# Weight group 3 rounded one step earlier, and last outputs stored as whole rows, in a two-layer decoder step

## The chip, the cores and the metric

The kernel runs on one core of a Trainium2 chip. The metric is device time of one execution in microseconds (us), the median over runs; lower is better. The engines are TensorE (PE in the profile; its weight loads are PEld), VectorE (DVE), ScalarE (ACT), GpSimd (POOL) and SyncE (SP), each with its own instruction queue in order. DMAs are issued from the queues of SP, ACT and POOL and run on 16 DMA engines.

## The reference

One inference step of a two-layer decoder, for two groups of requests that use the same weights: a prompt of 1024 tokens with 16 meta tokens ahead of it, and 8 samples of 8 tokens with state and cache. Layer one is an mLSTM, layer two an attention with forget gates; each is followed by a SwiGLU FFN, and a root-mean-square norm ends it. Everything is in f32. Cut to what matters here, the mixer's projection and the end:

```python
def rmsnorm(x, g):
    r = lax.rsqrt(jnp.mean(x * x, axis=-1, keepdims=True) + EPS)
    return x * r * g

def mlstm_mixer(xn, ..., w_in, b_ig, b_fg, mh_g, w_out):     # xn = rmsnorm(h, norm_a)
    p = xn @ w_in              # (T, 1024) @ (1024, 3088)
    q = heads(p[..., :HK]) * DK_A ** -0.5                    # HK = 512
    k = heads(p[..., HK:2 * HK])
    v = heads(p[..., 2 * HK:2 * HK + HV])                    # HV = 1024
    og = p[..., 2 * HK + HV:2 * HK + 2 * HV]
    gi = p[..., 2 * HK + 2 * HV:2 * HK + 2 * HV + H_A]       # gate columns, H_A = 8
    gf = p[..., 2 * HK + 2 * HV + H_A:]
    ...

def run_trunk(h, ...):
    for l in range(DEPTH):
        h = h + mixer_l(rmsnorm(h, ...))
        h = h + swiglu(rmsnorm(h, norm_ffn[l]), w_gate_up[l], w_down[l])
        ...
    y = rmsnorm(h, norm_final)
    return y, ...              # y_prompt is (1, 1024, 1024)
```

## The kernel before

All 1104 tokens (64 of the samples, 16 meta tokens, 1024 of the prompt) are held with features on the partitions, in nine tiles: tile 0 has the 80 first tokens, tiles 1 to 8 have 128 tokens of the prompt each (`TT`). Every product is made of three matmuls: each f32 operand is split into a high part, rounded to the f32r format by a cast on ACT, and a low part, the remainder, subtracted on DVE (`split`, lines 270 to 272; `mm3`, lines 191 to 195). So a weight has to be loaded, cast on ACT and subtracted on DVE before TensorE can use it.

**The start** is `values_a` (line 632): the value columns of `w_in`, in four groups `c` of 256 columns. The order of PE, SP, DVE and ACT is written out by hand there. A group is loaded in two halves `z` of 512 rows each (`fetch`, two raw buffers, tag `wraw`), and each half is split by `halve(c, z, ks)`, whose `ks` are those of its four blocks of 128 rows that are to be done: for each block one cast on ACT that also multiplies by the norm's gain (line 665) and one multiply-subtract on DVE (line 666). Group 3 also carries the 16 gate columns, so it is 272 columns wide; the gate columns of a half are split behind its last block (line 669, by the helper in lines 271 and 272). A product `values(c, i)` of group `c` and tile `i` has eight k-steps of three matmuls; the first four read half 0, the last four half 1, with the gate columns.

The first loop runs over steps `i` from 0 to 13 (`LAG` is 5). In a step, as far as tiles are left, TensorE makes group 0's product of tile `i`, then the eight transposes of tile `i + 2` (line 733); from step 5 on it then makes group 3's product of tile `i - 5`. ACT casts tile `i + 2`, writes out the product of group 0 with the factor `rr` (line 683), squares tile `i + 2` and takes its root (lines 751 and 752). DVE makes the low parts of tile `i + 2` (line 272) and copies its transposes (`keep`, line 745, four buffers `hs`, stored by POOL's queue), then a reciprocal for the next step (line 773). Loads of `x` tiles run ahead on SP's queue. Group 3's halves are loaded ahead of the loop and in step 0; `halve(3, ...)` stands behind the squares in steps 2 to 5, two blocks each. Group 1's loads, in step 5, take over group 3's raw buffers.

**The end** is `Tail` (line 2005): the last three tiles, 6 to 8, of the prompt. `finish` makes the last products of the second FFN, sums squares, transposes the three tiles back (feature blocks 0 to 3 into the PSUM tile `lo[x]`, blocks 4 to 7 into `hi[x]`), takes root and reciprocal for all three, and calls `out` for x = 0, 1, 2. `out` scales `lo` on DVE, with the final gain, and `hi` on ACT, and stores each of them. As place for the scaled outputs it uses the tile's own columns of `H`, where 512 features of a token lie as four pieces of 128, `T` = 1104 columns apart. All stores are issued on SP's queue.

Of the kernel before, what the change touches and what calls it, by code (L numbers as in the profile page):

```python
# [11 lines left out]
AF = mybir.ActivationFunctionType  # L12
ALU = mybir.AluOpType
# [4 lines left out]
P = 128  # L18
D = 1024
# [8 lines left out]
TT = [(0, T0)] + [(T0 + P * i, T0 + P * (i + 1)) for i in range(SEQ // P)]  # L28
# [603 lines left out]
def values_a(self, v, kp, gates, w_in, c3):  # L632

    nc, I = self.nc, self.I
    E = mybir.EngineType
# [6 lines left out]
    with ExitStack() as cw, self.pool("ppA0", bufs=4, space=PSUM) as pp:  # L642
# [3 lines left out]
        rr, ss = (xr.tile([P, NT], F32, name=nm, bufs=1) for nm in ("rr", "ss"))  # L646
# [3 lines left out]
        def fetch(c, z, queue=nc.sync):  # L650
            c0 = 2 * HA * DK + 256 * c
            raw = raws[c, z] = wr.tile([P, 4, 256], F32, name=self.uid("wraw"), tag="wraw", bufs=2)
            queue.dma_start(raw, w_in[4 * z * P : 4 * z * P + 4 * P, c0 : c0 + 256].rearrange("(k p) n -> p k n", p=P))

        def halve(c, z, ks=range(4)):
            raw = raws[c, z]
            n = 272 if c == 3 else 256
            hi, lo = W[c, z] = W.get((c, z)) or [wr.tile([P, 4 * n], F32R, name=self.uid(nm), tag=nm, bufs=4).rearrange(
                "p (k n) -> p k n", k=4) for nm in ("whi", "wlo")]
            if c == 2:  # L660
                self.split(raw, hi, lo)
                return
            for k in ks:
                y = hi[:, k, :256]
                nc.scalar.activation(y, raw[:, k], AF.Copy, scale=G(4 * z + k))
                nc.vector.scalar_tensor_tensor(out=lo[:, k, :256], in0=raw[:, k], scalar=G(4 * z + k),
                                               in1=y.bitcast(F32), op0=ALU.mult, op1=ALU.subtract)
            if c == 3 and ks[-1] == 3:
                self.split(gw[:, 4 * z : 4 * z + 4], hi[:, :, 256:], lo[:, :, 256:])

        def values(c, i, half=None):
            n, m = 272 if c == 3 else 256, size(i)
            ps = pp.tile([P, 512], F32, name=self.uid("tmps"), tag="mm0")
            for k in range(KT):
                if half and k == 4:
                    half()
                h, l = self.x_tile(i, k)
                wh, wl = W[c, k // 4]
                self.mm3(ps[:m, :n], h, l, wh[:, k % 4], wl[:, k % 4], k == 0, k == KT - 1)

            def out():
                r = 1.0 if c == 2 else rr[:m, i : i + 1]
                nc.scalar.activation(v(i)[:m, 2 * c : 2 * c + 2, :DV],
                                     ps[:m, :256].rearrange("p (h d) -> p h d", h=2), AF.Copy, scale=r)
                if c == 3:
                    nc.scalar.activation(gates[:m, i, :], ps[:m, 256:272], AF.Copy, scale=r)
            return out

        def reload(i):
            n, (t0, t1) = size(i), TT[i]  # L690
            y = hr[i] = xr.tile([P, KT, P], F32, name=f"hr{i}", tag="hr")
            nc.sync.dma_start(y[:, :, :n], self.hD[:, :, t0:t1])

        def spread(i):
            rb = xr.tile([P, P], F32, name=f"rb{i}", tag="rb")
            hr[i] = hr[i], rb
            nc.sync.dma_start(rb, rD[i].partition_broadcast(P))
# [21 lines left out]
        def load(i):  # L719
            x = xin[i] = cell(f"xin{i}")  # L720
            if i == 0:
                nc.sync.dma_start(x[:NS], I["x_sample"].rearrange("b t d -> (b t) d"))
                nc.sync.dma_start(x[NS:T0], I["meta_tokens"])
            else:
                nc.sync.dma_start(x, I["x_prompt"][0, (i - 1) * P : i * P, :])

        def turn(i):
            n = size(i)
            for g in range(2):
                ps = xps[i, g] = tp.tile([P, 4, P], F32, name=self.uid("xps"), tag="xps")  # L730
                for k in range(4):
                    f = 4 * g + k
                    nc.tensor.transpose(ps[:, k, :n], xin[i][:n, f * P : (f + 1) * P], self.ident[:n, :n])

        def halves(i):
            n, (t0, t1) = size(i), TT[i]
            for g in range(2):
                ks = slice(4 * g, 4 * g + 4)
                self.split(xps[i, g][:, :, :n], xh[:, ks, t0:t1], xl[:, ks, t0:t1])

        def keep(i):
            n, (t0, t1) = size(i), TT[i]
            hs = lp.tile([P, KT, P], F32, name="hs", bufs=4)
            for g in range(2):
                nc.vector.tensor_copy(hs[:, 4 * g : 4 * g + 4, :n], xps.pop((i, g))[:, :, :n])
            nc.gpsimd.dma_start(self.hD[:, :, t0:t1], hs[:, :, :n])

        def squares(i):
            n = size(i)
            x = xin.pop(i)[:n]  # L750
            nc.scalar.activation(x, x, AF.Square, accum_out=ss[:n, i : i + 1])
            nc.scalar.activation(rr[:n, i : i + 1], ss[:n, i : i + 1], AF.Sqrt, scale=1.0 / D, bias=self.eps[:n])
# [17 lines left out]
        for i in range(NT + LAG):  # L770
            if i < NT:
                out = values(0, i, None if i else lambda: turn(1))
                nc.vector.reciprocal(rr[: size(i), i : i + 1], rr[: size(i), i : i + 1])
            if i == 0:
                halves(1)
                nc.vector.tensor_tensor(out=gw, in0=gw, in1=self.gain[:, G_A : G_A + KT].unsqueeze(2).broadcast_to([P, KT, 16]),
                                        op=ALU.mult)
                rows = xr.tile([P, P], F32, name="growsF", tag="rb")[: NG - G_F]
                self.gains(rows)
                squares(1)  # L780
                keep(1)
                load(5)
                fetch(3, 1)
            if i + 2 < NT:
                turn(i + 2)
                halves(i + 2)
            if i < NT:
                out()
            if i + 2 < NT:
                squares(i + 2)  # L790
                keep(i + 2)
            if i + 6 < NT:
                load(i + 6)
            if 2 <= i < 6:
                halve(3, i // 2 - 1, range(2 * (i % 2), 2 * (i % 2) + 2))
            if i == 5:
                fetch(1, 0)
                fetch(1, 1)
                for x in range(3):
                    reload(x)  # L800
            if i == 7:
                ps = tp.tile([P, 4, P], F32, name="gpsF", tag="xps").rearrange("p a b -> p (a b)")
                nc.tensor.transpose(ps[:, : NG - G_F], rows, self.ident[: NG - G_F, : NG - G_F])
                nc.vector.tensor_copy(self.gain[:, G_F:], ps[:, : NG - G_F])
            if i == NT - 1:
                nc.gpsimd.dma_start(rD.rearrange("i p -> p i"), rr)
                for x in range(3):
                    spread(x)
            if 0 <= i - (NT + LAG - 3) < 2:
                halve(1, i - (NT + LAG - 3))  # L810
            if i >= LAG:
                values(3, i - LAG)()
# [69 lines left out]
@_add(Net)  # L882
def phase_a(self, vt):
    nc, I, O = self.nc, self.I, self.O
    w_in = I["w_in_a"][0]
    qkD = self.dram.tile([8, P, T], F32, name="qkD")
    ogD = self.dram.tile([8, P, T], F32, name="ogD")
# [1117 lines left out]
class Tail:  # L2005
# [57 lines left out]

    def out(self, x, lo, hi):
        net, i = self.net, DONE[3][x]
        nc, t0, t1 = net.nc, *TT[i]
        for g, ps in enumerate((lo, hi)):
            o = net.H[:, 4 * g : 4 * g + 4, t0:t1]
            y, rr = ps.rearrange("p (k n) -> p k n", k=4), self.r[:, 1, x : x + 1]
            if g:  # L2070
                nc.scalar.activation(o, y, AF.Copy, scale=rr)
            else:
                nc.vector.scalar_tensor_tensor(out=o, in0=y, scalar=rr, in1=net.sq[:, :512].rearrange(
                    "p (k n) -> p k n", k=4), op0=ALU.mult, op1=ALU.mult)
            nc.sync.dma_start(net.O["y_prompt"][0, (i - 1) * P : i * P, g * 512 : g * 512 + 512].rearrange(
                "p (k n) -> p k n", k=4), o)

    def finish(self, acc, groups):
        net = self.net
# [963 lines left out]
```

## Time and profile before

| | |
|---|---|
| median of 3 runs | 2831.09 us (2831.01 to 2832.83) |
| the profiled execution's own time | 2833.03 us |
| its span, first to last instruction | 2831.2 us |
| mean granted TensorE clock | 0.994 |
| busy: PE, DVE, ACT, POOL | 2760.9, 1797.8, 1177.0, 837.0 us |
| moved by DMA | 474.03 MB, mean 167 GB/s |

The profile has a page with sums, and views of the trace behind it: groups of instructions by line, waits (who waited for whom), a timeline in order of time (start in us from the span's start, length, engine, line, operation, output and inputs, count, and in brackets the idle time before it and what ended that), busy time in chosen stretches, and the DMAs. The end of a matmul is modelled, and neighbours overlap; the pace is read from starts. A "q" behind an engine's name marks its instruction queue.

### The profile page before, as it was taken

The numbers are of one execution on the slowest core, as the hardware profiler recorded it, in microseconds if no ns is written. First come the engines' busy times: TensorE is split into PE (matmuls) and PEld (weight loads), VectorE is DVE, ScalarE is ACT, GpSimd is POOL, SyncE is SP. The second block draws the span as 40 slices with busy tenths as digits, with TensorE's granted clock in tenths as the row PEclk, the third lists the DMA queues.
The fourth block names the chain that finished last, engine by engine and source line by source line (L and its number), as shares of the span: only waits on it lengthen the run. The fifth ranks groups of instructions, "written<-read, shape, count | busy, mean of one in ns | idle before, by whom it ended". The sixth has DMA issues, their size and how long they took to land. (4 is left out here: it accounts for less than half of the span.)

```text
span 2831.2 us, 60542 instructions
## 1 busy us (share of the span) xinstructions
PE 2760.9 (98%) x23543; PEld 2649.8 (94%) x23543; DVE 1797.8 (63%) x4025; ACT 1177.0 (42%) x2299; POOL 837.0 (30%) x1316
## 2 busy tenths in 40 slices
PE   8989999999999999999999999999999999999998
PEld 8989889999999999999999888777899999999998
DVE  4632565888887665563455444777388888765656
ACT  5422453432322333443444445777343323323345
POOL 3122233132332332124352202554313223323111
PEclk9989999999999999999999999999999999999999
DMA  6666547245554375545443676442524555527556
GB/s 197 170 186 172 144 125 254 91 145 164 174 172 144 115 247 171 194 143 174 139 170 131 234 277 227 153 143 86 157 80 131 175 174 165 161 90 233 182 194 214
DMA packets 438737, 474.03 MB, mean 167 GB/s; under 512 B 41158, under 2 KB 364994, under 8 KB 437426
## 3 DMA queue, kind: packets, MB, share of 16 engines
q1 hardware_dynamic: 388050, 321.30, 36.9%
q0 software_dynamic: 43904, 143.18, 15.3%
q10 hardware_dynamic: 6496, 5.68, 0.6%
q8 instruction: 185, 3.03, 0.5%
q14 instruction: 102, 0.84, 0.1%
HBM read 322.84 MB, written 147.21 MB: 166 GB/s over the span
## 5 line engine op out<-in xcount | busy, mean ns | idle before, releaser
L1614 PE MATMUL m<-xh,slot 128*128 128x276 f32 x2752 | 540.5, 290 | 1.8 <-ACT fs L1643 1.8
L1614 PEld LDWEIGHTS m<-xh,slot 128*128 128x128 f32 x2752 | 439.6, 188 | 3.6 <-ACT fs L1643 2.2
L1614 PE MATMUL m<-xl,slot 128*128 128x276 f32 x1376 | 397.1, 289 | 0.0
L1614 PEld LDWEIGHTS m<-xl,slot 128*128 128x128 f32 x1376 | 258.7, 188 | 0.0
L193 PE MATMUL tmps<-slot,xh 128*128 128x256 f32 (+2 forms) x864 | 243.1, 281 | 0.0
L195 PE MATMUL tmps<-slot,xl 128*128 128x256 f32 (+2 forms) x864 | 240.6, 278 | 0.0
L194 PE MATMUL tmps<-slot,xh 128*128 128x256 f32 (+2 forms) x864 | 240.5, 278 | 0.0
L272 DVE TENSOR_TENSOR slot<-slot,slot 128x1024 fp32r<-128x1024 f32 x124 | 162.7, 1313 | 61.3 <-ACT slot L271 59.6
L271 ACT CAST slot<-slot 128x1024 fp32r<-128x1024 f32 x124 | 129.5, 1045 | 140.9 <-PE m L1614 111.7
L194 PEld LDWEIGHTS tmps<-slot,xh 128*128 128x128 f32 (+1 forms) x864 | 159.2, 184 | 0.1
L195 PEld LDWEIGHTS tmps<-slot,xl 128*128 128x128 f32 (+1 forms) x864 | 158.6, 184 | 0.0
L193 PEld LDWEIGHTS tmps<-slot,xh 128*128 128x128 f32 (+1 forms) x864 | 158.4, 183 | 0.2
L193 PE MATMUL mmA<-xh,whi 128*128 128x384 f32 (+1 forms) x384 | 135.7, 353 | 0.0
L194 PE MATMUL mmA<-xl,whi 128*128 128x384 f32 (+1 forms) x384 | 128.6, 335 | 0.0
L195 PE MATMUL mmA<-xh,wlo 128*128 128x384 f32 (+1 forms) x384 | 128.2, 334 | 0.0
L272 DVE TENSOR_TENSOR slot<-vA,slot 128x1024 fp32r<-128x1024 f32 (+1 forms) x59 | 82.2, 1396 | 32.6 <-ACT slot L271 31.5
L272 DVE TENSOR_TENSOR slot<-Ht,slot 128x1024 fp32r<-128x1024 f32 (+1 forms) x59 | 82.0, 1393 | 32.7 <-ACT slot L271 31.6
L271 ACT CAST slot<-Ht 128x1024 fp32r<-128x1024 f32 (+1 forms) x59 | 60.9, 1036 | 95.5 <-PE m L1614 86.5
L271 ACT CAST slot<-vA 128x1024 fp32r<-128x1024 f32 (+1 forms) x59 | 60.8, 1035 | 95.5 <-PE m L1614 86.5
L1718 DVE TENSOR_TENSOR ws<-ws 128x128 f32<-128x128 f32 x264 | 93.7, 355 | 8.9
L2865 ACT ACTIVATE s<-s,nb 128x272 f32<-128x272 f32 (+7 forms) x126 | 98.9, 786 | 0.0
L2900 ACT COPY th<-tp 128x768 f32<-128x768 f32 (+1 forms) x80 | 73.6, 920 | 53.6 <-PE tp L2892 30.5
(808 smaller groups left out, 8665.9 us busy)
## 6 DMA issues: line engine op xcount, KB each, us to landing
ws<-in_w_down SPq DMA_DIRECT2D x176, 128.0 KB, 2.7
sD<-ws SPq DMA_DIRECT2D x176, 128.0 KB, 2.2
slot<-sD SPq DMA_DIRECT2D x40, 512.0 KB, 4.4
slot<-in_w_gate_up SPq DMA_DIRECT2D x36, 512.0 KB, 3.9
kp<-in_cache_k SPq DMA_DIRECT2D x32, 512.0 KB, 6.2
vp<-in_cache_v SPq DMA_DIRECT2D x32, 512.0 KB, 5.1
vA<-in_w_gate_up SPq DMA_DIRECT2D x26, 512.0 KB, 4.5
Ht<-in_w_gate_up SPq DMA_DIRECT2D x26, 512.0 KB, 3.9
```

What stands on the lines that cost most here:

```text
L193: mm(ps, sh, mh, start=first, stop=False)
L194: mm(ps, sh, ml, start=False, stop=False)
L195: mm(ps, sl, mh, start=False, stop=last)
L271: self.nc.scalar.copy(hi, src)
L272: self.nc.vector.tensor_tensor(out=lo, in0=src, in1=hi.bitcast(F32), op=ALU.subtract)
L1614: nc.tensor.matmul(u.ps[h, b], w[p][:, k], x[q][:, k], start=first and k == i == 0, stop=k == 3 and i == 2, skip_group_check=True)
L1718: tt(out=o, in0=a, in1=b, op=ALU.subtract)
L2865: nc.scalar.activation(ss[z, u], ss[z, u], AF.Exp, bias=nb[:, z : z + 1], accum_out=sm[:, u, z : z + 1])
L2900: nc.scalar.copy(th.rearrange("p x z (u h q) -> p h (x z u) q", h=2, q=64)[:, :, :n], pt[:, :, :n])
```

## The change

Two edits. In `values_a`, `halve(3, ...)` runs in steps 1 to 4 instead of 2 to 5, with the same blocks in the same order. In `Tail.out`, both halves of a tile's output are written side by side into row `x` of `H` (1024 neighbouring elements on each partition), and one DMA stores the whole rows of 4 KB; for x = 2 it is issued on ACT's queue. ACT's half is now issued ahead of DVE's. A line in `phase_a` only gives a name that nothing uses.

```diff
-            if 2 <= i < 6:
-                halve(3, i // 2 - 1, range(2 * (i % 2), 2 * (i % 2) + 2))
+            if 1 <= i < 5:
+                halve(3, (i - 1) // 2, range(2 * (1 - i % 2), 4 - 2 * (i % 2)))
...
 def phase_a(self, vt):
     nc, I, O = self.nc, self.I, self.O
+    E = mybir.EngineType
...
     def out(self, x, lo, hi):
         net, i = self.net, DONE[3][x]
-        nc, t0, t1 = net.nc, *TT[i]
-        for g, ps in enumerate((lo, hi)):
-            o = net.H[:, 4 * g : 4 * g + 4, t0:t1]
-            y, rr = ps.rearrange("p (k n) -> p k n", k=4), self.r[:, 1, x : x + 1]
-            if g:
-                nc.scalar.activation(o, y, AF.Copy, scale=rr)
-            else:
-                nc.vector.scalar_tensor_tensor(out=o, in0=y, scalar=rr, in1=net.sq[:, :512].rearrange(
-                    "p (k n) -> p k n", k=4), op0=ALU.mult, op1=ALU.mult)
-            nc.sync.dma_start(net.O["y_prompt"][0, (i - 1) * P : i * P, g * 512 : g * 512 + 512].rearrange(
-                "p (k n) -> p k n", k=4), o)
+        nc, rr = net.nc, self.r[:, 1, x : x + 1]
+        y = net.H[:, x, :D]
+        nc.scalar.activation(y[:, 512:], hi, AF.Copy, scale=rr)
+        nc.vector.scalar_tensor_tensor(out=y[:, :512], in0=lo, scalar=rr, in1=net.sq[:, :512], op0=ALU.mult, op1=ALU.mult)
+        (nc.scalar if x == 2 else nc.sync).dma_start(net.O["y_prompt"][0, (i - 1) * P : i * P], y)
```

## The prediction

> **What bounds the kernel now.** I read the page first, then TensorE's waits, then the timeline around the longest wait that the change can touch, then the clock in windows, and last the end of the trace.
>
> ```profile
> PE 2760.9 (98%) x23543; PEld 2649.8 (94%) x23543; DVE 1797.8 (63%) x4025; ACT 1177.0 (42%) x2299; POOL 837.0 (30%) x1316
> ```
>
> TensorE (PE) is busy for 98% of the span. Time can only come from its waits, from a lower granted clock, or from the two ends. Among its six longest waits of the whole run is this one (us in total, times, longest):
>
> ```profile
> PE tmps L193 <- ACT whi L271: 2.7, 1, 2.7
> ```
>
> ```profile
> 35.07 0.29 PE L195 MATMUL tmps<-whi,xl 128*80 128x272 f32 x1
> 38.11 0.51 PE L193 MATMUL tmps<-whi,xh 128*80 128x272 f32 x1 [2.75 <-ACT whi L271]
> ```
>
> The second row (start, length, instruction, idle before it) is the fifth k-step of the first product of weight group 3. It reads the second half of that group's weights, and the last write into that half is a narrow cast of the gate columns. ScalarE (ACT) makes it here, the third and, after the dots, the end of the fourth part of the group (columns: start, length):
>
> ```profile
> 33.54 0.90 ACT L665 ACTIVATE whi<-wraw,gain 128x256 fp32r<-128x256 f32 x2
> ...
> 37.83 0.23 ACT L271 CAST whi<-gw 128x64 fp32r<-128x64 f32 x1
> ```
>
> So TensorE arrives at 35.20 (one pace of 0.13 after 35.07) and finds the cast ending at 38.06. The wait also costs clock. In this table the columns are stretch, length, busy us (instructions) of PE, PEld, DVE, ACT, POOL, granted clock, DMA share, GB/s:
>
> ```profile
> 33.98:37.39 3.41, 1.38 (x11) 1.11 (x9) 3.32 (x7) 3.38 (x9) 0.84 (x1) 1.00 1.01 317
> 37.39:40.81 3.42, 2.69 (x11) 2.39 (x12) 1.12 (x5) 0.66 (x3) 0.85 (x1) 0.50 0.86 264
> 40.81:44.22 3.41, 3.41 (x18) 3.41 (x17) 0.00 (x0) 0.63 (x2) 0.00 (x0) 0.50 0.08 24
> 44.22:47.63 3.41, 3.41 (x30) 3.41 (x30) 0.98 (x2) 1.60 (x4) 0.00 (x0) 1.00 0.65 182
> 255.84:259.26 3.42, 1.93 (x13) 1.64 (x11) 0.71 (x2) 0.49 (x1) 3.42 (x7) 1.00 0.29 77
> 259.26:262.67 3.41, 2.78 (x23) 2.81 (x24) 1.39 (x4) 0.00 (x0) 3.41 (x5) 1.00 0.37 90
> ```
>
> After a window in which TensorE was busy 1.38 of 3.41 us (40%) the clock fell to 0.50 for two windows; after one with 1.93 of 3.42 (56%) it did not fall.
>
> **Part 1: the weights one step earlier.** The four calls of `halve(3, ...)` go from steps 2 to 5 to steps 1 to 4. Each issues two casts on ACT and two multiply-subtracts on DVE; the second and the fourth also split the gate columns. None issues a DMA. Nothing is added or removed.
>
> What the wait costs in this execution comes from the transposes, which start each step's second part:
>
> ```profile
> 25.59 1.04 PE L733 MATMUL xps<-ident,xin 128*128 128x128 f32 x8
> 29.20 1.04 PE L733 MATMUL xps<-ident,xin 128*128 128x128 f32 x8
> 32.82 1.04 PE L733 MATMUL xps<-ident,xin 128*128 128x128 f32 x8
> 45.39 1.04 PE L733 MATMUL xps<-ident,xin 128*128 128x128 f32 x8
> ```
>
> ```profile
> 64.41 0.48 ACT L683 ACTIVATE vA<-tmps,rr 128x256 f32<-128x256 f32 x1 [2.39 <-PE tmps L195]
> ...
> 67.44 0.48 ACT L683 ACTIVATE vA<-tmps,rr 128x256 f32<-128x256 f32 x1 [2.39 <-PE tmps L195]
> ```
>
> A step of transposes and one plain product is 32.82 - 29.20 = 3.62; a product of group 3 is 67.44 - 64.41 = 3.03. At full clock the last transposes would start at 32.82 + 3.62 + 3.03 = 39.47; they start at 45.39. The stall costs 5.92: 2.75 of wait, about 3.2 of half clock.
>
> Will the weights be there at 35.20? Step by step, ACT and DVE before:
>
> ```profile
> 21.43 0.29 ACT L752 ACTIVATE rr<-ss,eps 128x1 f32<-128x1 f32 x1
> 22.52 1.08 ACT L271 CAST xh<-xps 128x512 fp32r<-128x512 f32 x2 [0.80 <-PE xps L733]
> ```
>
> ```profile
> 23.14 1.29 DVE L272 TENSOR_TENSOR xl<-xps,xh 128x512 fp32r<-128x512 f32 x2 [1.06 <-ACT xh L271]
> 25.96 1.29 DVE L745 COPY hs<-xps 128x512 f32<-128x512 f32 x2 [1.53 <-DMA hD<-hs]
> ...
> 31.44 1.29 DVE L272 TENSOR_TENSOR xl<-xps,xh 128x512 fp32r<-128x512 f32 x2
> ...
> 34.07 0.88 DVE L666 SCALAR_TENSOR_TENSOR wlo<-wraw,gain,whi 128x256 fp32r<-128x256 f32 x2
> ```
>
> In step 1, ACT ends its root at 21.72 and idles 0.80 for the transposes; the new pair of casts takes 0.90, so that idle time hides nearly all of it and the casts of the next tile start about 0.1 late. VectorE (DVE) has 1.06 idle there and takes the pair (0.88) with the reciprocal behind it. If that cover were gone, each step would carry 0.9 more, and TensorE would wait those 0.9 at the second half. In step 2 the gate split adds some 0.15 on each engine; DVE's wait for a store until 25.96 stays. In steps 3 and 4 the pairs are in their old places, only a half further on. So the last pair is made where the third is now, from 33.54, with the gate cast behind it: high parts at about 34.6, low parts at 34.07 + 0.88 + 0.15 = 35.1. TensorE needs them at 35.20 and 35.33. I take a residual wait of 0.1 (bounds 0 and 1.0: one late DVE step), too short for a cold window. TensorE's PSUM and the transposes' buffers are let go by copies that move by no more than these 0.15. In step 5 the engines have one pair less. The queue on SP waits behind these casts for the raw buffers, so group 1's first load may start about 4 us earlier and share the DMA with stores; ACT first touches group 1 long after:
>
> ```profile
> 67.97 1.70 ACT L665 ACTIVATE whi<-wraw,gain 128x256 fp32r<-128x256 f32 x4
> ```
>
> What is late next? The plain product that follows needs tile 6, whose low parts end at 31.44 + 1.29 = 32.7, some 4 us ahead, so nothing.
>
> Does the gain last? From 40 to 400 us TensorE's longest waits are these:
>
> ```profile
> PE rps L1101 <- ACT lf L1103: 7.1, 1, 7.1
> PE nps L1441 <- POOL C L1398: 2.1, 1, 2.1
> PE tmps L195 <- DVE xl L711: 0.3, 1, 0.3
> ```
>
> None is for a DMA; chains between engines that follow TensorE's products move along with it.
>
> **Price in the median run.** The profiled execution took 2833.03 (span 2831.2), the median 2831.09: 1.94 less, near one window at half clock (3.41 / 2 = 1.7). Here the second cold window came because the first was busy for only 2.69 of 3.42; elsewhere 2.78 of 3.41 counted as enough. So the median run may have had one cold window fewer at this place (stall 4.2) or at another (5.9). I take 4.7, bounds 2.75 (no cold window) and 5.9.
>
> The Trainium skill ("TensorE: Matmul & The Clock Gate", "Part 1: The HAM clock gate") says that the clock is halved after an idle window of about 3.4 us and that windows run freely, not from the kernel's start. The second half supports a price that varies by run; by the first, a wait of 2.75 would cost no clock, and the gain here would be 2.65; the trace disagrees, at 40% busy.
>
> **Part 2: the last stores.** Six stores of 256 KB become three of 512 KB; two go out on SP's queue, the last on ACT's.
>
> ```profile
> 2822.35 1.84 ACT L2071 ACTIVATE Ht<-fin,tr 128x512 f32<-128x512 f32 x3 [0.24 <-DVE tr L2062]
> 2822.42 2.07 DVE L2073 SCALAR_TENSOR_TENSOR Ht<-fin,tr,sq 128x512 f32<-128x512 f32 x3
> 2823.06 4.13 SPq L2075 DMA_DIRECT2D out_y_prompt<-Ht  x6
> ```
>
> ```profile
> DMA packets 3169, 1.58 MB, mean 132 GB/s; under 512 B 96, under 2 KB 3168, under 8 KB 3168
> ```
>
> ```profile
> 2824.00:2829.50 5.50, 0.00 (x0) 0.00 (x0) 0.48 (x1) 0.19 (x1) 0.00 (x0) 0.50 1.00 284
> 24.00:32.00 8.00, 8.00 (x72) 8.00 (x72) 6.47 (x15) 7.00 (x17) 2.10 (x3) 1.00 1.02 387
> ```
>
> The engines compute for 2 us; then the DMA is full for 5.5 us at 284 GB/s, in pieces of 1.58 MB / 3168 = 500 bytes. The row of the start (loads and stores in whole rows) has 387 GB/s. At that rate 1.57 MB take 4.06. The first store now needs both halves of its row: DVE's first ends at 2823.1, so it starts about 0.15 later, data from 2824.15 instead of 2824.0. The third is issued by ACT when DVE ends at 2824.49, its data can start 0.94 behind, at 2825.4, and the DMA is at the second store until 2826.85 by then, so it never runs dry. End of data 2828.2 instead of 2829.5: gain 1.3. Bounds: -0.15 if the rate stays 284, 1.6 if the rate is a tenth higher. The new rows lie over columns of `H` that the transposes read, but TensorE runs these in order, and the last ones, which the output needs anyway, come behind all that read the overwritten rows.
>
> A rule against this part: the Trainium skill ("DMA: Bandwidth & Descriptors", "Specifications") puts line rate at 512 bytes and up, so longer rows would gain nothing; the two rows above speak against it.
>
> **Sum.** Profiled execution: 5.92 - 0.1 + 1.3 = 7.1, giving 2825.9. Median: 4.7 - 0.1 + 1.3 = 5.9, giving 2825.2.
>
> **The rivals.** (a) The median run pays no clock at this wait: 2.65 + 1.3 = 4.0, 2827.1; for it, the 56% row; against it, the 40% row. (b) The stores stay at 284 GB/s: 4.7 - 0.1 - 0.15, so 2826.6; this is the case in which that edit does nothing of what it says. (c) The gain of part 1 is given back at the 7.1 wait, if its chain hangs on a load and not on TensorE: 1.3 remains, 2829.8; against it, the rows above show no wait of TensorE for a DMA. (d) Slower: the raw weights come too late for step 1.
>
> ```profile
> 15.88 0.39 SPq L653 DMA_DIRECT2D wraw<-in_w_in_a  x1
> ```
>
> ```profile
> wraw<-in_w_in_a SPq DMA_DIRECT2D x5, 512.0 KB, 4.2
> ```
>
> Issued at 15.88, with the median of 4.2 they land at 20.1, and ACT asks at 21.7. If they took over 5.8, ACT would stand in front of the next tile's casts. That tile's low parts end at 24.43 today and its product starts behind the transposes of 25.59, at 26.5: 2.0 of slack. At 11 us they land at 26.9, 5.2 late, so TensorE waits 3 there and, as I estimate, 1.5 more at the second half, with two cold windows (3.4): 7.9 against 4.7 today, 2831.09 + 3.2 - 1.3 = 2833.0.
>
> **How the numbers follow.** A measurement of this kernel can tell about 0.2%, 5.7 us, from no change. Forecast 0.68: the bounds of the clock and of part 2 spread it from 2823.3 to about 2827, and 2825.2 stands just beyond the 5.7, so I put 0.52 of it there and 0.16 short of it. (a) 0.08, (b) 0.08, (c) 0.07, (d) 0.09. The range 2823.0 to 2830.0 takes in all but (d) and the ends of the forecast. Faster by over 0.2%: 0.52; within: 0.16 + 0.08 + 0.08 + 0.07 + 0.03 of (d) = 0.42; slower: 0.06, a still later load in (d).
>
> **What would show it.** Right: no wait of TensorE on line 271 near 35, clock 1.00 through 37 to 44, the transposes of tile 8 at about 39.6; three stores at the end and over 350 GB/s behind them, data over by 2828.5. Wrong: a new wait for casts near 26 (case d), a longer wait than 7.1 at line 1101 (c), or 284 GB/s at the end (b).

## The result, and the profile after

| | before | after |
|---|---|---|
| median of 20 runs each | 2829.78 us (2823.23 to 2833.84) | 2821.36 us (2817.62 to 2828.02) |
| the profiled execution | 2833.03 us, span 2831.2 | 2823.49 us, span 2821.7 |
| mean granted clock of the profiled execution | 0.994 | 0.995 |

The ratio is 0.9974 (0.9968 to 0.998): 7.4 us faster, between 5.7 and 9.1. The means of the twenty runs differ by as much, the two medians by 8.42. The three runs of before that the forecast started from had a median of 2831.09; twenty have 2829.78, and they spread over 10 us.

The page of after, first line of its busy times:

```profile
PE 2759.0 (98%) x23543; PEld 2648.7 (94%) x23543; DVE 1800.0 (64%) x4025; ACT 1177.0 (42%) x2299; POOL 838.0 (30%) x1316
```

The same number of instructions on each engine as before, and PE still at 98%: nothing was taken out of the work. What went are idle time and half clock. TensorE's longest waits of the whole run, in order (us in total, times, longest), no longer have the one on line 271 among them:

```profile
PE rps L1102 <- ACT lf L1104: 7.3, 1, 7.3
PE sp L2833 <- DVE mx L2837: 7.1, 16, 0.9
```

The place itself, in the timeline of PE, around the fifth k-step of the first product of group 3, and the transposes on either side of that product:

```profile
33.09 1.04 PE L733 MATMUL xps<-ident,xin 128*128 128x128 f32 x8
...
34.97 0.29 PE L195 MATMUL tmps<-whi,xl 128*80 128x272 f32 x1
35.09 0.29 PE L193 MATMUL tmps<-whi,xh 128*80 128x272 f32 x1
...
39.70 1.04 PE L733 MATMUL xps<-ident,xin 128*128 128x128 f32 x8
```

The row at 35.09 is the one that started at 38.11 before, behind 2.75 of idle time. It now follows its neighbour by the usual 0.12. The transposes come 6.61 after the previous ones (39.70 - 33.09); before it was 12.57 (45.39 - 32.82). In the windows (stretch, length, busy us and instructions of PE, PEld, DVE, ACT, POOL, granted clock, DMA share, GB/s) the clock stays at 1.00 where it was 0.50:

```profile
33.98:37.39 3.41, 3.41 (x30) 3.41 (x29) 3.32 (x8) 3.38 (x10) 0.85 (x1) 1.00 1.03 329
37.39:40.81 3.42, 3.42 (x32) 3.42 (x32) 0.26 (x2) 0.88 (x3) 0.86 (x1) 1.00 0.81 219
40.81:44.22 3.41, 3.41 (x30) 3.41 (x29) 2.56 (x5) 2.72 (x8) 0.37 (x1) 1.00 1.04 269
```

The end: the last reciprocal of before, then the timeline of after and a window of the stretch in which little but the stores is left:

```profile
2822.14 0.17 DVE L2062 RECIPROCAL tr<-tr 128x3 f32<-128x3 f32 x1 [1.95 <-ACT tr L2061]
```

```profile
2814.31 0.18 DVE L2063 RECIPROCAL tr<-tr 128x3 f32<-128x3 f32 x1 [1.95 <-ACT tr L2062]
2814.52 1.84 ACT L2069 ACTIVATE Ht<-fin,tr 128x512 f32<-128x512 f32 x3 [0.24 <-DVE tr L2063]
2815.40 0.99 SPq L2071 DMA_DIRECT2D out_y_prompt<-Ht  x2
2816.73 0.36 ACTq L2071 DMA_DIRECT2D out_y_prompt<-Ht  x1
```

```profile
2816.20:2820.00 3.80, 0.00 (x0) 0.00 (x0) 0.44 (x1) 0.17 (x1) 0.00 (x0) 0.53 1.01 404
```

Six issues became three, and the DMA, still full, moves 404 GB/s instead of 284. From the last reciprocal's end to the end of the span it takes 7.20; before it took 8.92. So 1.72 came from the tail.

To see where in the run the rest was gained, the same TensorE instruction was looked up in both traces (the order on PE is the same) and the starts subtracted. Before minus after is -0.28 us at 30 us, 5.7 at 60, 6.1 at 130 and still 6.1 at 300, 5.8 from 500 to 1570, 7.1 at 2750, 7.8 at 2815, and 9.5 at the end of the span. Part 1 is paid out at once and stays; the tail adds its own 1.7. The 1.9 in between, from 1570 to 2815, is not from an edited place. Around 1612 before had the first three of these waits, 2.2 in all; in the same stretch, around 1606, after has the last one alone, 0.6:

```profile
PE po L2606 <- DVE o L2601: 1.2, 1, 1.2
PE ktp L2549 <- DVE kT L2550: 0.8, 1, 0.8
PE ktp L2549 <- DMA kp<-in_cache_k: 0.2, 1, 0.2
...
PE ktp L2544 <- DMA kp<-in_cache_k: 0.6, 1, 0.6
```

Nor does the clock drop at the same places in the two executions. Executions of kernels that are the same differ like this: rows_one_queue, half_rows and cut_rows below run what after runs up to the tail, and at 2815 they are 7.9, 12.3 and 11.7 ahead of before, after 7.8.

### The profile page after: what moved, and what is told of

Its sections match the earlier page's. It is cut to its first block, busy times and chain, and to the rows that moved or that the text cites. A ratio compares the mean times of both kernels' runs of the same rounds, so it can differ in the third digit from the quotient of the medians.

```text
span 2821.7 us, 60540 instructions
## 1 busy us (share of the span) xinstructions
PE 2759.0 (98%) x23543; PEld 2648.7 (94%) x23543; DVE 1800.0 (64%) x4025; ACT 1177.0 (42%) x2299; POOL 838.0 (30%) x1316
```

## The experiments

Each ratio is to runs of before on the same chip. In the first four (30 runs of before, median 2829.62) the question is what each half of the change is worth, whether the clock is a price of its own, and whether the earlier weights are short of time. The last four ask about the stores and about the 7.1 wait. The three on the stores are one run each: they are read from their traces, and their times (2823.43, 2819.34 and 2821.79) lie within those of after's twenty runs and say nothing. The last one has 9 runs of before beside it, median 2830.07.

**part1: the weights alone.** The edit of `values_a` without that of `Tail.out`.

```diff
-            if 2 <= i < 6:
-                halve(3, i // 2 - 1, range(2 * (i % 2), 2 * (i % 2) + 2))
+            if 1 <= i < 5:
+                halve(3, (i - 1) // 2, range(2 * (1 - i % 2), 4 - 2 * (i % 2)))
```

> The first edit alone (group 3 rounded in steps 1 to 4; the stores as before). Theory: the gain of the front is the wait of TensorE at the second half of group 3 and the half clock behind it, whatever the end does. Then no wait of TensorE near 35 us, the transposes of tile 8 at 39.5 to 39.9, and the median 4.2 to 6 us below the kernel before. Rival: the two edits act on one another, or a good part of the gain lies in the middle of the run; then this kernel gains under 3 us while its front still shows 6.

Median 2824.8 of 11 runs, ratio 0.9984 (0.9975 to 0.9992): 4.5 us faster (2.3 to 7.1). The timeline of PE, around the product:

```profile
33.10 1.03 PE L733 MATMUL xps<-ident,xin 128*128 128x128 f32 x8
...
39.71 1.04 PE L733 MATMUL xps<-ident,xin 128*128 128x128 f32 x8
```

6.61 again, and the tail is 8.91, as before. The stall is gone with this edit alone.

**part2: the stores alone.** The edit of `Tail.out` without that of `values_a` (the lines that it adds; it removes those shown under the change).

```diff
+        y = net.H[:, x, :D]
+        nc.scalar.activation(y[:, 512:], hi, AF.Copy, scale=rr)
+        nc.vector.scalar_tensor_tensor(out=y[:, :512], in0=lo, scalar=rr, in1=net.sq[:, :512], op0=ALU.mult, op1=ALU.mult)
+        (nc.scalar if x == 2 else nc.sync).dma_start(net.O["y_prompt"][0, (i - 1) * P : i * P], y)
```

> The second edit alone (whole rows stored, the front as before). Theory: the end shortens by 1.7 us (reciprocal to last instruction 8.9 before, 7.2 after), and the median by as much, 1.3 to 1.8, less than the spread of single runs; the wait near 35 us is there again, 2.5 to 3.0, with 0, 1 or 2 windows of half clock behind it depending on where the wait lies in the windows. Rival (part of the rest of the gain comes from the end, by later work): over 3 us.

Median 2826.02 of 10 runs, ratio 0.9987 (0.9977 to 0.9997): 3.7 us faster (0.8 to 6.5). The stall is there as in before:

```profile
32.78 1.04 PE L733 MATMUL xps<-ident,xin 128*128 128x128 f32 x8
...
37.86 0.52 PE L193 MATMUL tmps<-whi,xh 128*80 128x272 f32 x1 [2.54 <-ACT whi L271]
...
45.22 1.04 PE L733 MATMUL xps<-ident,xin 128*128 128x128 f32 x8
```

12.44 between the transposes, and the tail is 7.20: in the trace the edit is worth 1.72, which lies inside the interval of the medians. The 3.7 of the medians is more than the 1.3 to 1.8 that was expected, and more than the 3 of the rival, but it is no evidence of a second effect; the interval is too wide.

**keep_busy: the wait without the half clock.** Before, with 26 matmuls of 224 columns, of which nothing is used, ahead of the fifth k-step. They stand where TensorE waits, so they should add no time. They write, each as a sum of its own, into the bank in which the product of group 3 and tile 0 is being summed, and that product does not keep its value in this kernel: it shows times only. All instructions of before are still there.

```diff
+                if c == 3 and i == 0 and k == 4:
+                    for y in range(26):
+                        nc.tensor.matmul(ps[:m, 288:512], self.x_tile(0, 0)[0], W[0, 0][0][:, y % 4, :224], start=True,
+                                         stop=True, skip_group_check=True)
```

> The kernel before, with 26 needless matmuls of 128x224 in front of the fifth k-step of the first product of group 3, into columns of its PSUM bank that nothing reads; they fill the wait and leave it as long as it is. Theory: the clock pays for half of the stall. Then the clock stays 1.00 from 35 to 45, the transposes of tile 8 start at 42.2 to 42.7 instead of 45.4, and the median is 1.5 to 3 us below before. Rival (the clock falls for another reason, or its price is hidden by other waits): the clock falls all the same, or the transposes come at 42.5 but the median stays within 1 us of before.

Median 2827.62 of 12 runs, ratio 0.9992 (0.9983 to 1.0): 2.3 us faster (0 to 4.8), with 26 instructions more. PE in the timeline, and the windows across the place:

```profile
33.19 1.04 PE L737 MATMUL xps<-ident,xin 128*128 128x128 f32 x8
...
35.57 2.82 PE L679 MATMUL tmps<-whi,xh 128*80 128x224 f32 x26
...
42.76 1.03 PE L737 MATMUL xps<-ident,xin 128*128 128x128 f32 x8
```

```profile
37.00:40.50 3.50, 3.44 (x31) 3.20 (x30) 1.45 (x5) 1.28 (x5) 0.85 (x1) 1.00 0.88 265
40.50:44.00 3.50, 3.50 (x33) 3.50 (x32) 0.00 (x0) 0.96 (x4) 0.00 (x0) 1.00 0.28 69
```

The weights come as late as before, TensorE does something instead of nothing, and the clock stays at 1.00. Nor is this a lucky place of the windows: counted back in steps of 3.41 from this run's first fall, at 151.57, one window reaches from 35.52 to 38.93, and almost the whole wait would have lain in it. The transposes are 9.57 apart. So the 12.57 of before divide: 9.57 - 6.61 = 2.96 for the late weights, 12.57 - 9.57 = 3.00 for the clock.

**two_earlier: another step ahead.** Both edits, and `halve(3, ...)` in steps 0 to 3.

```diff
-            if 1 <= i < 5:
-                halve(3, (i - 1) // 2, range(2 * (1 - i % 2), 4 - 2 * (i % 2)))
+            if i < 4:
+                halve(3, i // 2, range(2 * (i % 2), 2 * (i % 2) + 2))
```

> Both edits, but group 3 rounded in steps 0 to 3, two steps earlier than before. Its raw weights land at about 20.4, and ScalarE would ask for them at about 18. Theory (the load is the limit): ScalarE stands 2 to 2.5 us for the load in step 0, the casts of tile 3 start that much later, at about 21.3 instead of 18.9, and TensorE either has that much slack or waits up to 1 us near 22 to 26; median 0 to 3 us above the kernel with both edits as they are. Rival (earlier is better, the halves free buffers sooner): as fast or faster, no new wait of TensorE between 20 and 36.

Median 2821.88 of 7 runs, ratio 0.9971 (0.996 to 0.9982): the same as the change. ACT does run into the load, in its timeline:

```profile
20.43 0.91 ACT L665 ACTIVATE whi<-wraw,gain 128x256 fp32r<-128x256 f32 x2 [1.47 <-DMA wraw<-in_w_in_a]
21.25 1.05 ACT L271 CAST xh<-xps 128x512 fp32r<-128x512 f32 x2
```

The raw weights are there at 20.4, near the 20.1 of the forecast; ACT waited 1.47 where 2 to 2.5 were expected. The next tile's cast starts at 21.25, and TensorE does not wait for it. The expected loss did not come: the slack ahead of TensorE covers 1.47. In the kernel with the change, ACT asks at 21.98 and does not wait; by this run's 20.4 that is about 1.5 us after the data are there.

**rows_one_queue: is it the other queue?** Both edits, all three stores on SP's queue.

```diff
-        (nc.scalar if x == 2 else nc.sync).dma_start(net.O["y_prompt"][0, (i - 1) * P : i * P], y)
+        nc.sync.dma_start(net.O["y_prompt"][0, (i - 1) * P : i * P], y)
```

> Both edits, but the third store of whole rows goes out on SP's queue like the others. Before, the time from the last reciprocal's end to the last instruction was 8.92 us, with both edits 7.20. Theory (the size of the pieces sets the end): 7.15 to 7.35, since SP is free again when VectorE ends. Rival (the second queue matters): 7.6 or more.

In one profiled run the tail is 7.14, against 7.20.

```profile
2815.30 1.65 SPq L2071 DMA_DIRECT2D out_y_prompt<-Ht  x3
```

In this one pair of traces ACT's queue brings nothing.

**half_rows: is it the number of stores?** Both edits, but each tile's output stored by two DMAs in halves of a row, pieces of 2 KB, six stores on SP's queue.

```diff
-        (nc.scalar if x == 2 else nc.sync).dma_start(net.O["y_prompt"][0, (i - 1) * P : i * P], y)
+        for g in range(2):
+            nc.sync.dma_start(net.O["y_prompt"][0, (i - 1) * P : i * P, g * 512 : g * 512 + 512], y[:, g * 512 : g * 512 + 512])
```

> The outputs lie side by side as in the change, but each half row is stored by itself: six stores of 256 KB in pieces of 2 KB, all on SP's queue. Theory (size of the pieces): over 350 GB/s while the DMA is full, and 7.2 to 7.6 us from the last reciprocal to the end. Rival (the number of stores, each with its issue on SP): 8.5 to 9.0, near the kernel before.

The tail is 7.50. The issues, and the window in which the stores run alone:

```profile
2810.74 3.11 SPq L2072 DMA_DIRECT2D out_y_prompt<-Ht  x6
```

```profile
2812.00:2815.00 3.00, 0.00 (x0) 0.00 (x0) 0.15 (x1) 0.00 (x0) 0.00 (x0) 0.50 1.01 382
```

Six stores again, and still 382 GB/s.

**cut_rows: is it the size of the pieces?** Both edits, three stores on the two queues, but the outputs stand in the tile's old place, so that each store is again made of pieces of 512 bytes.

```diff
-        y = net.H[:, x, :D]
+        t0, t1 = TT[i]
+        y = net.H[:, :, t0:t1]
...
+        (nc.scalar if x == 2 else nc.sync).dma_start(net.O["y_prompt"][0, (i - 1) * P : i * P].rearrange("p (k n) -> p k n", k=8), y)
```

> Three stores of 512 KB, two on SP's queue and the third on ScalarE's, but the outputs lie in the tile's own columns of H as before, in pieces of 512 bytes. Theory (size of the pieces): 280 to 290 GB/s while the DMA is full, 8.8 to 9.2 us from the last reciprocal to the end, no better than before. Rival (number of stores): 7.2 to 7.6.

The tail is 9.27, 0.35 more than before and a little over the 9.2 that was expected; what the 0.35 is was not tried. Issues and window:

```profile
2811.47 1.30 SPq L2073 DMA_DIRECT2D out_y_prompt<-Ht  x2
2812.80 0.63 ACTq L2073 DMA_DIRECT2D out_y_prompt<-Ht  x1
```

```profile
2813.00:2818.00 5.00, 0.00 (x0) 0.00 (x0) 0.00 (x0) 0.00 (x0) 0.00 (x0) 0.51 1.00 283
```

With three stores and two queues the rate is that of before. It is the size of the pieces: 283 GB/s at 512 bytes, 382 at 2 KB, 404 at 4 KB. Single traces are enough for this, because the tail repeats: 8.91 to 8.92 in the three profiles with the old stores (before, part1, keep_busy), 7.19 or 7.20 in the four with the new ones (after, part2, two_earlier, loads_later).

**loads_later: the next stall of the same kind.** After the change, the longest wait of TensorE is at line 1102, 7.28 long. The traces of after around it, ACT and then SP's queue and PE:

```profile
147.34 1.04 ACT L259 CAST whi<-wraw 128x1024 fp32r<-128x1024 f32 x1 [9.73 <-DMA wraw<-in_w_in_a]
148.68 0.78 ACT L1104 COPY lf<-rps 8x336 f32<-8x336 f32 x2
```

```profile
124.61 18.17 SPq L1014 DMA_DIRECT2D cp<-in_cache_logf  x32
142.89 0.39 SPq L256 DMA_DIRECT2D wraw<-in_w_in_a  x1
```

```profile
149.14 0.80 PE L1102 MATMUL rps<-ident,lf_tm 128*8 128x128 f32 x3 [7.28 <-ACT lf L1104]
```

The wait is put down to ACT's copy `lf`, but the copy is short. ACT stood 9.73 at a cast of weights, in front of it in its own order, and the weights' load had been issued only at 142.89, behind 32 loads of pages of cached forget values on SP's queue. The experiment keeps both edits and begins those page loads later in the same stage:

```diff
-                next(pages, None)
+                if x >= 6:
+                    next(pages, None)
                 if x == 14:
+                    for _ in pages:
+                        pass
                     self.cache_prep(*self.cache, rpp, "r")
```

> Both edits, and in the stage behind the values the loads of the 32 pages of cached forget values are asked for from the seventh product on instead of from the first. With both edits TensorE waits 7.28 us near 142 us, for ScalarE's copies that stand behind a cast, which waits for a weight load that stands behind the 32 page loads on SP's queue; the clock is then at half for two or three windows, some also near 175. Theory: with 12 page loads in front of it instead of 32 the weight load lands at about 140, the wait falls under 1.5 us, the clock stays 1.00 to 165 us, and the median is 6 to 11 us below the kernel with both edits, near 2812 to 2816. Rival (the chain of the forget values itself is that long): the wait stays over 4 us and moves, and the median gains under 3. Second theory under test, that single runs spread by windows of half clock: with these windows gone the mean granted clock goes up by about 0.002.

Median 2813.98 of 5 runs (2812.59 to 2818.2), ratio to before 0.9948 (0.9934 to 0.9961): 14.7 us (11.0 to 18.7). It beats both kernels: the change alone had 0.9974 (0.9968 to 0.998), and the intervals do not meet. SP's queue and ACT in its timeline, then TensorE's wait there:

```profile
124.46 7.42 SPq L1017 DMA_DIRECT2D cp<-in_cache_logf  x12
131.99 0.39 SPq L256 DMA_DIRECT2D wraw<-in_w_in_a  x1
```

```profile
137.86 1.05 ACT L259 CAST whi<-wraw 128x1024 fp32r<-128x1024 f32 x1
141.76 0.78 ACT L1107 COPY lf<-rps 8x336 f32<-8x336 f32 x2
```

```profile
PE rps L1105 <- ACT lf L1107: 0.3, 1, 0.3
```

The load goes out 10.9 earlier, ACT does not wait at that cast, and TensorE's wait shrinks from 7.3 to 0.3. The stretch 134 to 184, first of after, then of this kernel:

```profile
134.00:184.00 50.00, 42.52 (x231) 41.32 (x230) 20.55 (x30) 14.00 (x21) 10.42 (x19) 0.83 0.59 179
```

```profile
134.00:184.00 50.00, 49.28 (x290) 47.62 (x289) 21.78 (x31) 17.03 (x25) 12.78 (x23) 0.97 0.71 208
```

Again two prices for one late load: idle time, and clock (0.83 against 0.97). The clock stays at 1.00 to 167.1, as expected; over the whole run its mean over the five runs is 0.9968, against 0.9955 over the twenty of after, 0.0013 more where 0.002 was expected.

## Why the prediction was right or wrong

**Where it was wrong.** The forecast time, 2825.2, and the lower end of the range, 2823.0, were too high; 2821.36 lies 1.64 below the range. The direction was right, and the gain nearly so: 5.9 us were forecast, 7.4 (5.7 to 9.1) were measured. The step that failed is "Price in the median run". It took the median of three runs as the base of the time, and read the 1.94 between it and the profiled execution as one window of half clock at this very place. Both were more than three runs can carry:

- The base was 1.31 too high (2831.09 for 2829.78), and nothing in the range allowed for it: all its bounds were bounds of the gain. With the base of the twenty runs the same sum gives 2823.9 and the range begins at 2821.7, 0.33 above the measured median; the 0.42 by which the tail's term was too small (below) is more than that, so the two together cover the miss.
- The price of the stall was cut from 5.92 to 4.7 on that reading. Its ground, that a first window with 2.69 of 3.42 busy lets a second one follow and 2.78 of 3.41 would have been enough, does not hold: the row with 2.78 is a window at full clock, and the clock can stay at half even behind a window that is busy throughout (the rows from 174.50 and 177.91 in the last section). Whether 4.7 itself was too low, the runs do not settle. part1, with this edit alone, gained 4.5 (2.3 to 7.1). The granted clock of every run points the same way: (1 - clock) times the span, the time lost to half clock, has a mean of 15.5 us over the 30 runs of before beside part1 and of 13.3 over part1's 11, 2.1 less with a standard error of about 0.8; the mean time without it falls by 2.5, near the wait of 2.75. Both profiles that have the stall, of before and of part2, have both cold windows, but these begin at nearly the same place, 37.39 and 37.37, so the two are hardly two samples.

Of the 3.84 between 2825.2 and 2821.36, then, 1.31 is the base, 0.42 the tail's term and 0.1 a wait that did not come. The other 2.0 has no place that the runs show: about half of it is the difference between the medians' 8.42 and the ratio's 7.4, and the rest is less than the 1.7 by which the measured gain is uncertain.

Two slips of the prediction's working changed little. The bounds of its terms reach down to 2831.09 - 5.9 - 1.6 = 2823.6, not to 2823.3. And its 500 bytes are a mean over 96 packets under 512 bytes; the pieces of the stores are 512 bytes (3072 of them make 1.57 MB).

**The weights.** The working of this part held to a tenth or two. Forecast: high parts at 34.6, low parts at 35.1, a residual wait of 0.1, transposes of tile 8 at about 39.6. Measured: ACT's gate cast 34.34 + 0.23 = 34.57, DVE's 34.87 + 0.22 = 35.09, no wait, 39.70. In the timelines of ACT and DVE of after:

```profile
21.77 0.29 ACT L752 ACTIVATE rr<-ss,eps 128x1 f32<-128x1 f32 x1
21.98 0.90 ACT L665 ACTIVATE whi<-wraw,gain 128x256 fp32r<-128x256 f32 x2
22.89 1.08 ACT L271 CAST xh<-xps 128x512 fp32r<-128x512 f32 x2
...
33.55 0.89 ACT L665 ACTIVATE whi<-wraw,gain 128x256 fp32r<-128x256 f32 x2
34.34 0.23 ACT L271 CAST whi<-gw 128x64 fp32r<-128x64 f32 x1
```

```profile
34.07 0.88 DVE L666 SCALAR_TENSOR_TENSOR wlo<-wraw,gain,whi 128x256 fp32r<-128x256 f32 x2
34.87 0.22 DVE L272 TENSOR_TENSOR wlo<-gw,whi 128x64 fp32r<-128x64 f32 x1
```

The new pair at 21.98 fills the idle time of 0.80 that was there. This execution was 0.34 behind already at the root (21.77 for 21.43); from there to the next tile's casts it takes 1.12 (22.89 - 21.77), against 1.09 before (22.52 - 21.43). So the pair costs 0.03 in that place, where 0.1 was forecast.

**The clock.** That a wait of 2.75 has a price of its own in clock is shown by keep_busy: about 3.0 at this place. The Trainium skill ("TensorE: Matmul & The Clock Gate", "Part 1: The HAM clock gate") lets the clock fall after an idle window of about 3.4 us; by that, a wait of 2.75 would have cost none. The traces disagree: the clock fell to 0.50, and the transposes are 12.57 apart with the wait idle and 9.57 with it filled.

**The stores.** Gain 1.3 forecast, 1.72 measured. The rate was taken from the row of the start, 387; it is 404, which is worth 0.17 of the 0.42 (1.57 MB in 3.89 us instead of 4.06). Where the rest comes from is open; even the upper bound, 1.6, was too low. The reason given, the size of the pieces, is the right one by cut_rows, half_rows and rows_one_queue. The rule of the Trainium skill that 512 bytes are enough for the full rate ("DMA: Bandwidth & Descriptors", "Specifications") does not hold for these stores: 283 GB/s at 512 bytes. Two parts of the edit, the queue of ACT and the smaller number of stores, bring nothing that these runs show: 7.14, 7.20 and 7.50 lie together, 8.92 and 9.27 apart from them.

**The rivals.** (a), no price in clock, falls with keep_busy. (b), stores at 284, falls with the row of 404. (c), a gain given back at line 1101, falls in part only: before and after differ by 6.1 on either side of it, so nothing was given back. But the reason against it, that no wait of TensorE there is for a load, was wrong: the chain does hang on a load, through ACT. It did not matter here because the load's place behind the page loads moved along with the rest (142.89 for 149.05). (d), weights too late for step 1, fell too, with room: about 1.5 us in the change, and two_earlier, which uses that room up, loses nothing measurable.

**What stays open.** The sum of the two halves by their medians, 4.5 and 3.7, is 8.2, against 7.4 for both; within the intervals. By their clocks, part2's runs lost 13.0 us to half clock, 2.5 less than before's, with a standard error of 1.3, though its profile has the stall and both cold windows. Up to 0.9 of it belongs to the tail, which runs at half clock and became 1.72 shorter; the rest may be chance, since the clocks are given to 0.001 (2.8 us) and the runs are ten. Nor can the runs tell whether the 1.9 us that the two profiled executions differ by between 1570 and 2815 belong to the change: executions that run the same instructions there, on one chip, lie 4.4 apart (rows_one_queue at 7.9, half_rows at 12.3).

## What to carry to other kernels

A wait of TensorE may have to be paid twice, as idle time and as half clock behind it; the distance between two instructions on either side of it shows both, and filling the wait with needless matmuls separates them. Where a wait is put down to a short instruction, look at what stood in front of that one on its engine, and then at the queue on which the load for it was issued: an early prefetch may be all that holds it. And before a few microseconds are forecast, take the spread of the runs into the range: with three runs within 2 us, twenty may still spread over 10.

## What the runs showed of the hardware

- The rate of stores from SBUF to DRAM depends on the piece far beyond 512 bytes: 283 GB/s at 512 bytes, 382 at 2 KB, 404 at 4 KB, with the DMA full in each case.
- Executions that run the same instructions differ by whole windows of half clock. rows_one_queue and half_rows are the same up to the tail and ran on one chip; in the one's profile the clock falls at 143.8, 174.6, 1737.9 and 2120.2, in the other's at 146.0, 251.8 and 1576.1, for one or more windows of 3.41 each. The mean clocks of after's twenty runs lie between 0.993 and 0.997; the one with 0.993 has a span of 2826.2, the four with 0.997 have 2817.0 in the mean.
- The clock also falls without a long idle time, and can stay down behind a window that is busy throughout. These are three windows of after; in the first, TensorE is busy for 94% (its ends are modelled), and among its work are matmuls of 8x8:

```profile
171.09:174.50 3.41, 3.21 (x25) 2.71 (x23) 1.43 (x3) 1.34 (x2) 0.55 (x1) 1.00 0.87 261
174.50:177.91 3.41, 3.41 (x13) 3.34 (x13) 0.44 (x3) 0.15 (x1) 0.00 (x0) 0.50 1.06 351
177.91:181.33 3.42, 3.42 (x12) 3.42 (x11) 1.07 (x1) 0.00 (x0) 0.00 (x0) 0.50 0.34 84
```

The same fall behind a window that is busy for 94% is in six of the ten profiles, before among them (at 180.8). So the busy share of one window does not foretell the clock here. Whether the small matmuls count for little in what the clock goes by was not tried.
